# Row gathers of layer 0 recorded at other places: fewer beside the latent heads' inverses and second scan, more beside the dense experts and the attention projections

## The chip, the core and the metric

The kernel runs on one core of a Trainium2 chip. The metric is device microseconds (us) of one execution; the median of three executions is 4625.11 us (4613.94 to 4629.98). The program has five instruction streams: TensorE (PE, with its weight loads PEld), VectorE (DVE), ScalarE (ACT), GpSimd (POOL) and SyncE (SP). Each stream runs its instructions in the order in which they stand; streams wait for each other by semaphores.

## The reference

Two layers over 512 latent tokens and 256 context tokens, width 1024. Layer 0 mixes with a bidirectional gated DeltaNet, layer 1 with windowed attention, and each ends with a PEER expert retrieval:

```python
for i in range(DEPTH):
    y, yc = gdn_mixer(...) if i % 2 == 0 else swa_mixer(...)
    x = x + g1 * y
    x = x + g2 * peer_ffn(modulate(x, ...), w_query, sub_keys, expert_u, expert_v)
    if not last:
        xc = xc + cg1 * yc
        xc = xc + cg2 * peer_ffn(modulate(xc, ...), ...)
return rmsnorm(x, final_g)

def peer_ffn(h, ...):              # 8 heads x 16 experts = 128 of 16384 experts for each token
    idx, gate = top_k(...)         # from two products with 128 sub-keys each
    act = gelu(einsum('pkd,pd->pk', expert_u[idx], h)) * gate
    return einsum('pk,pkd->pd', act, expert_v[idx])
```

## The kernel before

Tokens stand in tiles of 128: two of context, four of latents. The experts of a tile are computed in one of two ways. **Dense** tiles (three of layer 0, two of layer 1) run through all 16384 experts as matrix products: `ups` makes `pu` (lines 84 to 86, three matmuls for one product because weights are split into a high and a low part), `dense` multiplies by gate tables `G` and makes `pv`. The split of a weight tile is a cast on ACT (line 295, `wh`) and a subtraction on DVE (line 296, `wl`). Dense work goes in 16 **superblocks**: each has eight products `pu` (the last two superblocks have none, since `pu` runs 16 products ahead) and 16 weight tiles of `pv`, and ends with six adds into `acc` (line 1328).

**Gathered** tiles (both context tiles and one latent tile of layer 0, two of layer 1) fetch the chosen experts only. One gather is an indirect DMA of 128 rows, 512 KB, issued by POOL. A tile needs 128 gathers of `u` (line 1184; each is multiplied with the tokens by one DVE instruction, line 1186) and then 128 of `v` (line 1211). Four `v` gathers make a **group**: DVE builds a selection `W` (line 1204) and PE adds the four into `po` by eight matmuls (line 1218; the profiler shows 16). When a tile's last group is done, `finish` copies `po` to `gacc` (line 1223), scales it, adds it to the stream `xf` (lines 1132 and 1133) and stores it to `xl` in memory (line 1135). The second context tile's `v` are two works, of 20 and of 12 groups (`CUT = 20`); the latent tile's come between them.

Gathers are recorded between other work: `self.back` lists gather works, and a call `self.tick(n, mix)` adds `n` to a debt and records gathers until the debt is paid, `u` and `v` by turns as `mix` says. The table `TICK` holds `n` for each place:

```python
self.tick(TICK["inv"][h0 // 4], MIX["inv"][h0 // 4])      # 8 times in each latent half
self.tick(TICK["scan"][h0 // 4], MIX["scan"][h0 // 4])    # 32 times in each latent half
self.tick(TICK["u", l], MIX["dense"])                     # before each of 112 products pu
self.tick(TICK["v", l], MIX["dense"])                     # 128 times, once for a weight tile of pv
self.tick(TICK["swa"], MIX["swa"])                        # attention projections, 6 per tile
done()                                                    # = drain: records all gathers that are left
norm(0, 2, 1)                                             # context tiles, before columns(4, ...)
```

A scheduler then orders all instructions by recording order and by when they can start. Recording order is a priority: a gather that found no free row buffer is put behind later work. There are six row buffers for both kinds (`RING`), five more in the dense stage of layer 0 (`MORE`).

The order of the program around the change: context heads, then the latent heads in two halves (`gdn_units`: gates and decay matrices, 31 steps of a block inverse on DVE at lines 574 and 576, inverse products at line 598, scan at lines 657 to 682), output projection (`gdn_out`, `py`), routing of four tiles (`peer_route`, `pq` and top-k), the first 16 products `pu`, gate tables (`gates_dram`, `pg`, line 1263), the dense stage, then attention (`swa`): norm of the latents, projections `pj`, norm of the context, scores.

Of the kernel before, what the change touches and what calls it, by code (L numbers as in the profile page):

```python
# [51 lines left out]
DELTA = 0  # L52
PIN = 1
ADA = 8
TICK = {"norm": 0, "proj": 0, "z": (0, 0), "mat": (0, 0), "inv": (4, 5), "scan": (1, 4), "out": 2, "swa": 6, "route": {"c": 0, "a": 0, "bf": 0, "b": 0}, "gates": (1, 2),
        ("u", 0): 2.1, ("v", 0): 1.9, ("u", 1): 2.2, ("v", 1): 2}

MIX = {"proj": "uv", "z": ("uv", "uv"), "norm": "uv", "mat": ("uv", "uv"), "inv": ("uv", "uv"), "scan": ("uv", "uv"), "out": "v", "swa": "v", "route": "v", "gates": "V", "dense": "uv"}

# [5 lines left out]
class Kern:  # L65
# [355 lines left out]
    def gdn_z(self, si, ns, hi, lo, p, ps, pt, bufs, raw):  # L421
# [5 lines left out]
        for n in ns:  # L427
            zw = [self.wsplit(p, A["g_z"][n, i], "w", [4, 256], raw, 2) for i in range(2)]
            for t in range(NT):
                pz = ps.tile([128, 512], F32, name="pz", tag=pt, bufs=bufs)[:, 0:256]  # L430
                for k in range(KT):
                    s = slice(t * 128, (t + 1) * 128)
                    zh, zl = zw[k // 4]
                    self.mm3(pz, hi[:, k, s], lo[:, k, s], zh[:, k % 4, :], zl[:, k % 4, :], k == 0, k == KT - 1)
                self.tick(TICK["z"][ns[0] // 2], MIX["z"][ns[0] // 2])
                zz = p.tile([128, 2, 128], F32, name="zz", tag="zz", bufs=2)
# [51 lines left out]
    def gdn_units(self, si, h0, HB, S, OD, side, ps, tags):  # L488
# [30 lines left out]
        with ExitStack() as c2:  # L519
            pr = c2.enter_context(self.pool(f"gr{si}{h0}", side))  # L520
            KQ = load(self.KQ, "kq", pr, 2)
            for gi in range(HB // NH):
# [9 lines left out]
                def decay(d, lm, rm, neg):  # L532
                    rr = pr.tile([128, 4, 128], F32, name="rr", tag="rr", bufs=2)
                    for i, h in enumerate(heads):
                        for t in range(NT):
                            nc.scalar.mul(rr[:, i * NT + t, :], rm, V["g"][:, t, 8 * d + h:8 * d + h + 1])
                    pe = bank("pe", "pe")
                    mm(pe, lm, rr, start=True, stop=False)
                    mm(pe, self.identb, neg[:, None, :].to_broadcast([128, 4, 128]), start=False, stop=True)
                    E = pr.tile([128, 4, 128], F32, name="E", tag="E", bufs=2)  # L540
                    nc.scalar.activation(E, pe, AF.Exp)
                    return E
# [9 lines left out]

                self.tick(TICK["mat"][h0 // 4], MIX["mat"][h0 // 4])
                Ef = decay(0, self.m_gt, self.m_le, self.neg_gt)
# [29 lines left out]
        with ExitStack() as c2:  # L584
# [5 lines left out]
            for g4 in range(NU // 4):  # L590
# [9 lines left out]

                self.tick(TICK["inv"][h0 // 4], MIX["inv"][h0 // 4])
                D4, a4, b4 = ([X[:, u, :] for u in us] for X in (Dm, ta, tb))
# [29 lines left out]
        for step, hh in [(st, hg + i) for hg in range(0, HB, 4) for st in range(NT) for i in range(4)]:  # L632
            h = h0 + hh
            for d in range(2):
                t = step if d == 0 else NT - 1 - step
                u = d * (NU // 2) + hh * NT + t
                inv = (tb if d == 0 else ta)[:, u, :]
                self.tick(TICK["scan"][h0 // 4], MIX["scan"][h0 // 4])
                s = slice(t * 128, (t + 1) * 128)
# [90 lines left out]
    def out_proj(self, wsrc, gate, p, ps, pt, bufs, resident, plain=False):  # L730
# [11 lines left out]
        def run(tiles):  # L742
# [3 lines left out]
            for n in range(4):  # L746
# [3 lines left out]
                for x, (y, _, xout) in zip(xs, tiles):  # L750
                    py = ps.tile([128, 512], F32, name="py", tag=pt, bufs=bufs)[:, 0:256]
                    for k in range(KT):
                        self.mm(py, [i[:, k] for i in y], [w[:, k % 4, :] for w in W[n][k // 4]], k == 0, k == KT - 1)
                    self.tick(TICK["out"], MIX["out"])
                    gy = p.tile([128, 256], F32, name="y", tag="oy", bufs=3)
# [8 lines left out]
    def swa(self, xl, gate, xout, done, free):  # L764
# [3 lines left out]
        with ExitStack() as ctx:  # L768
# [6 lines left out]
            with ExitStack() as c1:  # L775
# [19 lines left out]
                def columns(n, tiles):  # L795
                    w = [self.wsplit(p, A["s_in"][n, i], "w", [4, 256], 2, 2) for i in range(2)]
                    Q = {}
                    for t in tiles:
                        s = slice(t * 128, (t + 1) * 128)
                        pj = ps.tile([128, 256], F32, name="pj", tag="pj", bufs=3)  # L800
                        for k in range(KT):
                            wh, wl = w[k // 4]
                            self.mm3(pj, hi[:, k, s], lo[:, k, s], wh[:, k % 4, :], wl[:, k % 4, :], k == 0, k == KT - 1)
                        self.tick(TICK["swa"], MIX["swa"])
                        if n == 5:
# [766 lines left out]
```

## Time and profile before

| | |
|---|---|
| median of 3 executions | 4625.11 us |
| profiled execution, its own time | 4615.7 us |
| its span, first to last instruction | 4613.9 us |
| PE, DVE, ACT, POOL busy | 84%, 68%, 39%, 38% |
| bytes moved by DMA | 1258.59 MB |
| of them by POOL's queue (gathers, mostly) | 712.07 MB |

Busy PE time is modelled and matmuls overlap, so 84% is not the share of a peak. What counts is the stage: from the latent heads to the attention projections the program passes through stretches in which DVE, PE or the DMA engines are full in turn.

### The profile page before, as it was taken

What the parts mean: (1) busy time and instruction counts of PE and PEld (TensorE: products, weight loads), DVE (VectorE), ACT (ScalarE), POOL (GpSimd) and SP (SyncE); (2) the same over time, 40 slices, a digit from 0 to 9 for tenths busy, and PEclk for the clock granted to TensorE, in tenths of its full rate; (3) what the DMA queues carried; (4) which work ended last, traced back from release to release, by engine and by line L of the source; (5) the groups of instructions that cost most, each with busy time, mean ns of one, the idle gap of its engine ahead of it and who ended that gap; (6) DMA issues with size and microseconds to landing.
All of it is one profiled execution on the core that took longest, in us unless ns stands there. A gap on an engine that the chain in (4) does not pass through costs nothing.

```text
span 4613.9 us, 65361 instructions
## 1 busy us (share of the span) xinstructions
PE 3888.7 (84%) x23123; PEld 3126.8 (68%) x23123; DVE 3153.7 (68%) x7853; ACT 1789.2 (39%) x3428; POOL 1749.3 (38%) x1463
## 2 busy tenths in 40 slices
PE   7989989647798879999999997897956778888997
PEld 5867778545577668777877775765845666666665
DVE  4663469976699888666853344665898996767634
ACT  4754563413235633322332223443336332333322
POOL 0000011654345362465643340000340766656553
PEclk9989999878899989999999998998978899999999
DMA  6725553768798997899988883201255999999998
GB/s 237 245 86 184 206 186 109 283 242 310 283 319 280 305 375 273 326 393 367 379 326 320 329 321 138 78 19 70 82 187 157 392 365 395 406 396 409 400 398 338
DMA packets 432904, 1258.59 MB, mean 273 GB/s; under 512 B 40640, under 2 KB 139840, under 8 KB 432576
## 3 DMA queue, kind: packets, MB, share of 16 engines
q0 software_dynamic: 195968, 712.07, 40.8%
q1 hardware_dynamic: 236608, 542.34, 32.9%
q8 instruction: 182, 2.98, 0.3%
q14 instruction: 146, 1.20, 0.1%
HBM read 1176.66 MB, written 77.59 MB: 272 GB/s over the span
## 4 chain that ended last, share of the span: by engine, by line
PE 47%; DVE 22%; DMA 12%; issue 7%; ACT 4%; POOL 2%; SPq 0%; DVEq 0%; ACTq 0%; POOLq 0%
PE pv L84 5%; PE pv L85 5%; PE po L1218 5%; DMA u<-p_u,idx 5%; PE pv L86 5%; DVE u L1186 4%; PE pu L86 4%; PE pu L84 4%; PE pu L85 4%; DVE wl L296 3%; DMA v<-p_v,idxT 3%; DVE oa L1254 1%; ACT wh L295 1%; PE pg L1263 1%; DVE ob L1261 1%
## 5 line engine op out<-in xcount | busy, mean ns | idle before, releaser
L1184 POOL DMA_INDIRECT u<-p_u,idx x640 | 844.3, 1319 | 712.8 <-DVE u L1186 157.2
L296 DVE TENSOR_TENSOR wl<-w,wh 128x1024 fp32r<-128x1024 f32 x604 | 737.0, 1223 | 422.1 <-ACT wh L295 411.8
L1211 POOL DMA_INDIRECT v<-p_v,idxT x640 | 729.9, 1140 | 747.2 <-PE po L1218 426.5
L295 ACT CAST wh<-w 128x1024 fp32r<-128x1024 f32 x636 | 659.2, 1046 | 885.9 <-PE pu L85 222.8
L1186 DVE SCALAR_TENSOR_TENSOR u<-u,hg 128x1024 f32<-128x1024 f32 x640 | 770.4, 1223 | 198.9 <-DMA u<-p_u,idx 196.3
L84 PE MATMUL pu<-lo,wh 128*128 128x384 f32 (+1 forms) x2048 | 658.4, 321 | 80.6 <-ACT a L1282 50.9
L86 PE MATMUL pu<-hi,wl 128*128 128x384 f32 (+1 forms) x2048 | 657.8, 321 | 48.3 <-DVE wl L296 43.0
L85 PE MATMUL pu<-hi,wh 128*128 128x384 f32 (+1 forms) x2048 | 650.6, 318 | 0.0
L84 PE MATMUL pv<-wl,ah 128*128 128x512 f32 x1280 | 525.0, 410 | 97.8 <-DVE wl L296 93.1
L85 PE MATMUL pv<-wh,ah 128*128 128x512 f32 x1280 | 510.4, 399 | 0.0
L86 PE MATMUL pv<-wh,al 128*128 128x512 f32 x1280 | 507.9, 398 | 0.0
L84 PEld LDWEIGHTS pu<-lo,wh 128*128 128x128 f32 x2048 | 407.0, 199 | 125.9 <-ACT a L1282 65.5
L86 PEld LDWEIGHTS pu<-hi,wl 128*128 128x128 f32 x2048 | 406.7, 199 | 65.9 <-DVE wl L296 54.6
L85 PEld LDWEIGHTS pu<-hi,wh 128*128 128x128 f32 x2048 | 406.5, 198 | 7.7 <-issue 6.7
L84 PEld LDWEIGHTS pv<-wl,ah 128*128 128x128 f32 x1280 | 246.5, 193 | 229.8 <-DVE wl L296 126.4
L1218 PE MATMUL po<-v,W 128*32 128x512 f32 x2560 | 322.7, 618 | 43.9 <-DMA v<-p_v,idxT 43.8
L86 PEld LDWEIGHTS pv<-wh,al 128*128 128x128 f32 x1280 | 246.2, 192 | 59.0 <-issue 4.2
L1282 ACT ACTIVATE a<-pu 128x384 f32<-128x384 f32 (+1 forms) x256 | 110.8, 434 | 442.0 <-PE pu L86 434.8
L96 ACT CAST ah<-a 128x384 fp32r<-128x384 f32 (+1 forms) x256 | 116.6, 460 | 422.3 <-PE pv L85 379.6
L85 PEld LDWEIGHTS pv<-wh,ah 128*128 128x128 f32 x1280 | 247.1, 193 | 49.0 <-issue 0.8
L296 POOL TENSOR_TENSOR wl<-w,wh 128x1024 fp32r<-128x1024 f32 x32 | 78.8, 2472 | 514.1 <-ACT wh L295 467.5
L1263 PE MATMUL pg<-oa,ob 128*128 128x128 f32 x1280 | 177.2, 293 | 56.8 <-DVE oa L1254 32.7
(485 smaller groups left out, 7139.2 us busy)
## 6 DMA issues: line engine op xcount, KB each, us to landing
w<-p_ut SPq DMA_DIRECT2D x256, 512.0 KB, 6.7
w<-p_vt SPq DMA_DIRECT2D x256, 512.0 KB, 6.8
w<-adaw SPq DMA_DIRECT2D x96, 512.0 KB, 5.4
G<-st SPq DMA_DIRECT2D x20, 2048.0 KB, 13.6
w<-g_qkv SPq DMA_DIRECT2D x48, 512.0 KB, 5.1
Gt<-G SPq DMA_DIRECT2D x32, 768.0 KB, 6.8
w<-p_wq SPq DMA_DIRECT2D x32, 512.0 KB, 5.7
Gt<-G SPq DMA_DIRECT2D x32, 512.0 KB, 6.8
```

The lines of the kernel that those rows point to most:

```text
L84: mm(out, lh, rl, start=start, stop=False)
L85: mm(out, lh, rh, start=False, stop=False)
L86: mm(out, ll, rh, start=False, stop=stop)
L96: self.nc.scalar.copy(hi, x)
L295: nc.scalar.copy(hi, w)
L296: (sub or nc.vector).tensor_sub(lo, w, hi)
L1184: nc.gpsimd.indirect_dma_start(out=u, out_offset=None, in_=A["p_u"], in_offset=bass.IndirectOffsetOnAxis(ap=idx[:, s:s + 1], axis=0))
L1186: pin(nc.vector.scalar_tensor_tensor(u, u, 1.0, h, op0=OP.mult, op1=OP.mult, accum_out=w[:, s:s + 1]))
L1211: nc.gpsimd.indirect_dma_start(out=v, out_offset=None, in_=A["p_v"], in_offset=bass.IndirectOffsetOnAxis(ap=idxT[:, t:t + 1], axis=0))
L1218: pin(nc.tensor.matmul(po[hf][32 * g:32 * g + 32, :], W[:, g, :], vs[g][:, hf * 512:(hf + 1) * 512], start=j == j0, stop=j == j1 - 1, tile ...
L1263: nc.tensor.matmul(pg[:, :, j], ob[:, j, :], oa[:, j, :], start=True, stop=True)
L1282: nc.scalar.activation(a.rearrange("p g t -> p (g t)"), pu, AF.Gelu)
```

## The change

Two lines of the table change. In the latent heads each tick of the inverse products asks for 3 and 3 gathers (4 and 5 before) and each tick of the scans for 1 and 2 (1 and 4 before). In the dense stage of layer 0 a `pu` asks for 2.2 (2.1) and a weight tile of `pv` for 2.1 (1.9). No arithmetic is added or removed, and the same 768 gathers of layer 0 are made.

```diff
-TICK = {"norm": 0, "proj": 0, "z": (0, 0), "mat": (0, 0), "inv": (4, 5), "scan": (1, 4), "out": 2, "swa": 6, "route": {"c": 0, "a": 0, "bf": 0, "b": 0}, "gates": (1, 2),
-        ("u", 0): 2.1, ("v", 0): 1.9, ("u", 1): 2.2, ("v", 1): 2}
+TICK = {"norm": 0, "proj": 0, "z": (0, 0), "mat": (0, 0), "inv": (3, 3), "scan": (1, 2), "out": 2, "swa": 6, "route": {"c": 0, "a": 0, "bf": 0, "b": 0}, "gates": (1, 2),
+        ("u", 0): 2.2, ("v", 0): 2.1, ("u", 1): 2.2, ("v", 1): 2}
```

The layer-0 ticks from the latent heads to the output projection ask for 72 + 160 + 32 = 264 gathers before and 48 + 96 + 32 = 176 after; those of the dense stage for 478 and 515.

Where the scheduler puts the instructions that use the rows was counted in both built programs. `u` are counted as DVE instructions of line 1186, groups of `v` as sets of eight matmuls of line 1218:

| place | `u` before | `u` after | groups before | groups after |
|---|---|---|---|---|
| latent heads, both halves | 128 | 128 to 130 | 1 | 0 |
| output projection | 15 | 6 to 8 | 3 | 5 |
| norm and routing, first 20 `pu` | 37 | 0 | 17 | 5 |
| gate tables | 0 | 0 | 11 | 12 |
| superblocks 0 and 1 | 67 | 35 | 0 | 8 |
| superblocks 2, 3, 4, 5 | 9, 15, 22, 22 | 25, 40, 20, 10 | 0, 3, 5, 6 | 2, 0, 0, 1 |
| superblocks 6, 7, 8 | 17, 24, 28 | 21, 21, 23 | 4, 2, 1 | 6, 5, 6 |
| superblocks 9, 10 | 0, 0 | 29, 24 | 8, 8 | 2, 2 |
| superblocks 11, 12, 13 | 0 | 0 | 8, 7, 9 | 9, 9, 8 |
| superblocks 14, 15 | 0 | 0 | 3, 0 | 4, 5 |
| attention projections | 0 | 0 | 0 | 7 |

The first place is POOL's stream around the second latent half (`ta`, `tb`, `X` are buffers of its inverse; `x_...` is a buffer of its inverse products). Before:

```order
L514 MEMSET ta 128x4096
L515 MEMSET tb 128x4096
L1184 DMA u<-p_u,idx 128x1024 x24
L566 MEMSET X 128x1024
L567 MEMSET X 128x32
L1184 DMA u<-p_u,idx 128x1024 x22
L589 MEMSET x_9042 128x512
```

And in the changed kernel:

```order
L514 MEMSET ta 128x4096
L515 MEMSET tb 128x4096
L1184 DMA u<-p_u,idx 128x1024 x24
L566 MEMSET X 128x1024
L567 MEMSET X 128x32
L1184 DMA u<-p_u,idx 128x1024 x12
L589 MEMSET x_9018 128x512
```

Ten gathers moved from the block inverse to behind the last row shown; from there to the first `v` there are 53 `u` before and 63 after, so the heads end with the same number.

The second place is DVE's stream in the routing: the top-k (`top`, `ti`, `wk`, `sc`) of one query product for four tiles, with the weight split `wl`. Before:

```order
L1004 MATCH_REPLACE wk<-top_11131,sc 128x128
L1005 MAX top_11130<-wk 128x8
L1186 SCALAR_TENSOR_TENSOR u,gw<-u,hg 128x1024
L1005 MAX top_11131<-wk 128x8
L1006 MAX_INDEX ti_11134<-top_11130,wk 128x8
L296 TENSOR_TENSOR wl<-w,wh 128x1024
L1006 MAX_INDEX ti_11135<-top_11131,wk 128x8
L1002 MAX top_11128<-sc 128x8
```

And in the changed kernel:

```order
L1004 MATCH_REPLACE wk<-top_10801,sc 128x128
L1005 MAX top_10800<-wk 128x8
L1005 MAX top_10801<-wk 128x8
L1006 MAX_INDEX ti_10804<-top_10800,wk 128x8
L1006 MAX_INDEX ti_10805<-top_10801,wk 128x8
L296 TENSOR_TENSOR wl<-w,wh 128x1024
L1002 MAX top_10798<-sc 128x8
```

No `u` product stands in the routing any more.

The third place is ACT's stream from the end of the dense stage into the projections: `gacc` is the second context tile's sum, `junk` the squares of the norm of a tile (`x_25208` and `x_25209` are the two context tiles in both programs), `Q`, `qT` copies of projections. Before:

```order
L1223 COPY gacc<-po 128x512 x2
L96 CAST ah<-a 128x384 x2
L295 CAST wh<-w 128x1024
L96 CAST ah<-a 128x384 x2
L295 CAST wh<-w 128x1024
L96 CAST ah<-a 128x384 x2
L295 CAST wh<-w 128x1024 x6
L255 ACTIVATE junk,ss<-x_24423 128x1024
L255 ACTIVATE junk,ss<-x_24424 128x1024
L255 ACTIVATE junk,ss<-x_25208 128x1024
L255 ACTIVATE junk,ss<-x_24425 128x1024
L255 ACTIVATE junk,ss<-x_25209 128x1024
```

And in the changed kernel:

```order
L809 COPY Q<-pj 128x256 x3
L1223 COPY gacc<-po 128x512 x2
L295 CAST wh<-w 128x1024
L809 COPY Q<-pj 128x256
L295 CAST wh<-w 128x1024
L837 COPY qT<-ptq 64x512 x2
L255 ACTIVATE junk,ss<-x_25209 128x1024
L257 ACTIVATE r<-ss,eps 128x2
L272 ACTIVATE hk<-pt,col_77 128x256 x2
```

The second context tile's sum moved from the dense stage behind the third copy of the fourth projection, and the norm that needs it stands a few instructions behind. On PE, 18 matmuls of `pj` and 8 transposes of `Q` stand between that tile's last group and the first transposes of the context norm; behind those come the projections of the context.

## Rows read from the trace of the kernel before

**Rows 1.** The page: busy time of the engines, and GB/s in 40 slices.

```profile
PE 3888.7 (84%) x23123; PEld 3126.8 (68%) x23123; DVE 3153.7 (68%) x7853; ACT 1789.2 (39%) x3428; POOL 1749.3 (38%) x1463
...
GB/s 237 245 86 184 206 186 109 283 242 310 283 319 280 305 375 273 326 393 367 379 326 320 329 321 138 78 19 70 82 187 157 392 365 395 406 396 409 400 398 338
```

**Rows 2.** Busy time of each engine in stretches of the program (us).

```profile
core 0: us, PE busy (x) PEld busy (x) DVE busy (x) ACT busy (x) POOL busy (x), PEclk, DMA share, GB/s
920.00:976.00 56.00, 14.08 (x96) 13.88 (x96) 49.47 (x106) 7.73 (x12) 24.56 (x20) 0.62 0.61 214
1018.00:1103.00 85.00, 59.19 (x373) 51.45 (x371) 76.22 (x204) 32.38 (x107) 47.80 (x40) 0.84 0.82 291
1103.00:1231.00 128.00, 85.71 (x408) 62.48 (x408) 64.28 (x145) 39.20 (x114) 41.32 (x41) 0.80 0.85 314
1231.00:1340.00 109.00, 104.28 (x538) 79.38 (x538) 96.64 (x444) 28.90 (x42) 52.37 (x50) 0.97 0.88 313
1340.00:1460.00 120.00, 118.59 (x715) 98.54 (x713) 117.70 (x550) 48.93 (x70) 64.38 (x48) 1.00 0.87 303
1460.00:1622.00 162.00, 128.21 (x950) 101.54 (x950) 138.60 (x377) 113.22 (x299) 65.04 (x45) 0.95 0.91 294
1622.00:1791.90 169.90, 128.75 (x605) 112.07 (x603) 139.01 (x224) 51.62 (x77) 101.66 (x74) 0.90 0.98 368
1791.90:1859.30 67.40, 65.73 (x326) 60.02 (x326) 64.15 (x159) 25.55 (x36) 0.57 (x1) 0.97 0.50 167
1791.90:2104.00 312.10, 296.04 (x1553) 244.89 (x1554) 227.44 (x407) 95.89 (x132) 149.18 (x123) 0.99 0.87 331
2104.00:2336.20 232.20, 218.98 (x1119) 186.81 (x1119) 176.59 (x265) 72.75 (x102) 140.33 (x102) 0.98 0.95 363
...
2336.20:2749.60 413.40, 413.40 (x2322) 315.84 (x2321) 169.44 (x233) 119.17 (x163) 161.16 (x166) 1.00 0.88 328
2749.60:2823.30 73.70, 71.16 (x333) 54.04 (x331) 33.41 (x41) 18.95 (x24) 11.17 (x21) 1.00 0.50 174
2789.70:2823.30 33.60, 31.77 (x141) 25.97 (x139) 12.91 (x15) 5.27 (x5) 7.01 (x14) 1.00 0.27 96
2823.30:2860.00 36.70, 6.21 (x32) 4.38 (x32) 16.44 (x22) 20.61 (x33) 0.00 (x0) 0.61 0.43 161
2860.00:2955.00 95.00, 92.16 (x733) 89.87 (x734) 50.62 (x187) 32.49 (x66) 0.00 (x0) 0.97 0.17 56
3224.80:3328.50 103.70, 102.48 (x493) 86.28 (x494) 76.86 (x484) 31.61 (x48) 34.93 (x15) 0.97 0.25 81
```

**Rows 3.** DVE's costliest groups from 1231 to 1460.

```profile
L296 DVE TENSOR_TENSOR wl<-w,wh 128x1024 fp32r<-128x1024 f32 x35 | 42.6, 1218 | 1.7 <-ACT wh L295 1.7
L1186 DVE SCALAR_TENSOR_TENSOR u<-u,hg 128x1024 f32<-128x1024 f32 x32 | 38.9, 1216 | 11.4 <-DMA u<-p_u,idx 11.4
```

**Rows 4.** The chain from 1460 to 1622: one group (start us, us).

```profile
1514.17 1.85 PE po L1218 x16
```

**Rows 5.** Waits from 1103 to 1231: total us, times, longest.

```profile
DVE u L1186 <- DMA u<-p_u,idx: 26.9, 10, 5.9
...
PE po L1218 <- DMA v<-p_v,idxT: 22.4, 2, 17.6
```

**Rows 6.** Gathers in the table of DMA issues: count, median us to landing.

```profile
u<-p_u,idx POOLq DMA_INDIRECT x640, 8.3
v<-p_v,idxT POOLq DMA_INDIRECT x640, 7.9
```

**Rows 7.** The chain from the last add of the dense stage into the norm.

```profile
2825.44 1.22 DVE acc L1132
...
2827.71 1.23 DVE xf L1133
...
2831.79 7.14 DMA x<-xl
...
2840.19 1.28 ACT L257
```

## The prediction

> **What bounds the kernel now.** The page first [rows 1]: PE is busy 84% of the span, DVE 68%, POOL 38%, and the GB/s line moves between 19 and 409. No engine is full all the time, so I read the stages one by one in the table of busy times by stretches [rows 2]. The program has a different limit in each.
>
> In the second half of the latent heads DVE is the limit: 49.5 of 56 us before the inverse products and 76.2 of 85 in the scan. In the output projection and the norm (1103 to 1231) nothing is full; the waits there [rows 5] are for gathers: 26.9 us of DVE for `u`, 22.4 us of PE for `v`, one of them 17.6. In the routing (1231 to 1460, 229 us) DVE and PE are both full: 96.6 + 117.7 = 214.3 and 104.3 + 118.6 = 222.9. Among DVE's costliest groups stand 32 `u` products, 38.9 us and 11.4 of waiting [rows 3]. In the gate tables DVE leads (138.6 of 162). In the dense stage PE leads: 413.4 of 413.4 in superblocks 9 to 13, 219.0 of 232.2 in 6 to 8, 296.0 of 312.1 in 2 to 5. In 6 to 8 the DMA share is 0.95 too. The attention projections are PE again, 92.2 of 95 us, with the DMA engines at 0.17.
>
> So rows cost a different engine in each place. A `u` is 1.22 us of DVE [rows 3], about 1.3 with what it adds between instructions (my choice). A group of `v` is 1.85 us of PE in the chain [rows 4]; the dense stage gives the same: superblock 2 has no group and takes 67.4, so (413.4 - 5 x 67.4) / 40 groups = 1.91 [rows 2].
>
> **The change part by part.** The counts are those of the table of places above. The heads end with the same number of rows; what leaves is the routing's share, and what gains is the dense stage and the projections.
>
> *Heads.* Ten `u` leave the block inverse, a place where DVE is nearly full: -13. They come in the scan, as full: +13. Sum 0, bounds -13 (the scan's 9 idle us hide most of them) to +6.
>
> *Output projection and norm.* Some eight `u` of 15 go, and with them part of 26.9 us of waits; two groups more come, and the long `v` wait stays, since POOL still issues the first `v` behind the last `u`. I take -6; bounds -15 (more than half of the `u` waits) and +3 (the two groups, with no wait saved).
>
> *Routing.* DVE's 214.3 us shed 32 x 1.3 = 42 and fall to about 172, and 11.4 of waits go too. PE becomes the floor. Layer 1's routing has the same matmuls without groups and takes 103.7, 102.5 of it PE [rows 2]. The 480 `pu` matmuls (20 products) are priced by the difference of a superblock with and without its 192: (67.4 - 33.6) / 192 = 0.176, so 84.5. Three groups that stay behind the norm are 5.7. Sum 194; with the loose ends of the present stage (229 - 223 = 6) some 199: **-30**. Bounds -15 (the `pu` still wait for `wl`, whose 35 subtractions stand in DVE's order) and -35 (the floor).
>
> *Gate tables.* 12 groups for 11, no `u`: 0.
>
> *Superblocks 0 and 1 with their lead* (1622 to 1791.9, 169.9 us; PE 128.8, DVE 139.0, DMA share 0.98): eight groups come (+15), 32 `u` go. This stretch waits for rows and tables, not for an engine, so fewer rows (67 before, 35 + 32 after) is no change in bytes. I take +3; bounds -10 and +10.
>
> *Superblocks 2 to 15* are the heart. PE's floors before are 296.0, 219.0, 413.4 and 71.2 [rows 2] against 312.1, 232.2, 413.4 and 73.7: 32 us of excess, 29 of it in the seven superblocks that hold all 137 `u`. That is 0.21 us of loss for a `u` on top of what hides beside PE. After the change the same stretch has 213 `u` and 59 groups instead of 64.
> - 2 to 5: 14 groups become 3 (-21), 68 `u` become 95. But they lump: superblock 3 gets 40, and DVE there needs 33 (a superblock of 9 to 13, with no `u`, takes it 169.4 / 5 = 34 with its groups' selections) + 40 x 1.3 = 85, over PE's 67; superblock 2 gets 25 and 4 gets 20, the latter beside the pair sums of routing, some 71 and 77 with the excess. With 69 for superblock 5 the sum is 302; the ring's waits add 8: 310, **-2**.
> - 6 to 8: 7 groups become 17, and rows 69 + 28 = 97 become 65 + 68 = 133. The window moved 363 GB/s x 232.2 us = 84.3 MB [rows 2]; 36 rows of 0.524 MB make it 103. The fastest slices of the page are 392 to 409 GB/s [rows 1], so 103 MB takes some 258 at 399: **+26**. The engines alone would give +19 (ten groups), or 0 if rows come early.
> - 9 and 10: 16 groups become 4 (-23), 53 `u` come (+13): **-10**.
> - 11 to 13: 24 groups become 26: **+4**. 14 and 15: 3 become 9: **+11**, as PE is full there (71.2 of 73.7).
>
> Sum about **+27** with rounding; bounds -10 (floor alone: 5 groups fewer at 1.91, `u` at nothing) and +45 (every lump at its worst).
>
> The Trainium skill, in "DMA: Bandwidth & Descriptors", section "Issuing engines are not separate DMA queues", says that transfers issued by different engines share the same 16 DMA engines and interleave there. By that rule gathers that move into the dense stage delay its weight tiles. The trace agrees so far: the DMA share there is 0.87 to 0.98 [rows 2], while the routing that loses rows has 0.87.
>
> The same page's section on bandwidth gives about 358 GB/s for a core's memory side; by that estimate 103 MB would take 288 us, 56 more than now. The trace disagrees: 363 over a whole window [rows 2].
>
> *Attention projections.* Seven groups more at 1.91 are +13, for PE is busy 92.2 of 95. Then the second context tile ends here and no longer before the norm. Its tail is a copy, scale and add (1.22 + 1.23), store and load (7.14), and squares, root and scale (1.28 and two more), all rows of the like tail of the latents [rows 7]: some 17 us. Behind its last group PE has 26 short instructions, at 92.2 / 733 = 0.126 each some 3.3, with their weights up to 6. So 11 us of waiting are new. The 28 rows themselves arrive by a ring of six with 7.9 to 8.3 us to land [rows 6]: five rings, most of it beside the norm (36.7 us, DMA share 0.43); I add 1. Sum **+25**; bounds +5 (the groups run in the norm, where PE is busy 6.2 of 36.7) and +32.
>
> Sum: 0 - 6 - 30 + 0 + 3 + 27 + 25 = **+19**. The profiled execution took 4615.7, so it would take 4635. The three runs lie 1.8 below to 14.3 above it; the mean of the four is 4621.2, and on that the changed kernel takes 4640.
>
> **The rivals.** (1) *Faster.* The excess of superblocks 2 to 8 belongs to the gathers' transfers and not to DVE, which is busy only 227 of 312 and 177 of 232 there. Then what counts there is how many rows PE waits for, the lumps of `u` lie beside PE's work, and the stretch goes with PE's floor (-10), and the sum is 0 - 6 - 30 + 3 - 10 + 25 = -18: 4603. For it: PE is busy 0.95 of 2 to 5 already with `u` beside it, and groups (1.9 us of the full engine) drop by five. Against it: the lumps of 40 and of 17 groups. It decides when the dense term is below some -6. (2) *No change.* The seven groups and the context's tail hide in the norm and in the first projections (term +5 rather than +25): sum 0, about 4621. For it: PE has 30 idle us in the norm; against it: PE's order has the last group behind the third part of the fourth tile's projections. (3) *Bound by the DMA engines.* The dense term is +45 and the routing gives only 22: 4665. For it: a share of 0.95 to 0.98 already; against it: superblocks 9 to 13, at 0.88 and 328 GB/s, lose rows of `v`.
>
> **How the numbers follow.** Runs of before differ by 0.3% (16 us), so that is about what can be told from no change: 13.9 us either way. Chances: the sum as worked out 0.33, the DMA case 0.18, no change 0.25, faster 0.24. Most of the first case is slower by more than 0.3%, part of it (0.07) within; its own range is 4625 to 4655. From these cases: slower 0.45, same 0.29, faster 0.26. The range runs from 4600 (the faster case) to 4670 (the DMA case).
>
> **What would show it.** In the profile after: the routing some 199 us long with no `u` and PE idle under 10 us; superblock 3 long (85) with DVE full; superblocks 6 to 8 at 258 with a DMA share over 0.95; the projections about 120 us with a wait of PE of 10 us or more ahead of the context's transposes. I am wrong if the routing stays at 229, which means that `wl` or weights set it and not the rows; if 2 to 8 take 528 or less, which is rival 1; or if the projections stay near 100.

## The result, and the profile after

The changed kernel takes 4650.36 us (median, 4646.31 to 4661.81) against 4625.11: a ratio of 1.0065, 95% interval 1.005 to 1.008. It is slower by some 30 us. Forecast were 4640 us, and slower with a chance of 0.45. The profiled execution has a span of 4644.5, 30.6 more than before.

The page of the changed kernel, against [rows 1]:

```profile
PE 3896.6 (84%) x23123; PEld 3130.6 (67%) x23123; DVE 3154.9 (68%) x7853; ACT 1786.2 (38%) x3426; POOL 1757.1 (38%) x1463
...
GB/s 247 243 89 191 218 161 104 306 214 331 250 109 231 337 376 351 311 310 388 378 363 348 333 322 229 114 19 69 82 191 143 377 381 384 400 409 409 386 408 328
```

The engines are as busy as before, to 8 us. Only the line of GB/s shows where the change is: the slice with 319 before, in the routing, has 109, and the two slices from the end of the dense stage on have 229 and 114 where 138 and 78 stood.

Busy time by stretches of the changed kernel, the same stages as [rows 2] (the second scan, output projection, routing, gate tables, superblocks 0 and 1, 2 to 5, superblock 3 alone, 6 to 8, 9 and 10, 11 to 13, 14 and 15, norm, projections):

```profile
core 0: us, PE busy (x) PEld busy (x) DVE busy (x) ACT busy (x) POOL busy (x), PEclk, DMA share, GB/s
...
1001.30:1098.00 96.70, 64.38 (x346) 54.42 (x345) 84.55 (x214) 32.08 (x103) 62.63 (x48) 0.80 0.85 308
1098.00:1218.50 120.50, 87.94 (x445) 62.93 (x443) 53.51 (x130) 39.95 (x115) 37.37 (x39) 0.84 0.86 318
1218.50:1415.70 197.20, 192.18 (x1043) 170.88 (x1043) 176.43 (x920) 76.38 (x112) 14.57 (x15) 0.99 0.44 145
1415.70:1578.60 162.90, 131.74 (x965) 103.43 (x966) 135.95 (x375) 111.13 (x295) 66.88 (x46) 0.93 0.87 283
1578.60:1751.50 172.90, 141.63 (x718) 111.77 (x717) 104.13 (x166) 51.00 (x76) 88.54 (x75) 0.90 0.95 362
1751.50:2055.80 304.30, 283.11 (x1402) 246.39 (x1400) 256.53 (x452) 97.64 (x135) 154.51 (x112) 0.97 0.86 324
1826.00:1911.20 85.20, 75.46 (x359) 67.73 (x359) 77.04 (x121) 23.92 (x33) 62.86 (x41) 0.92 0.98 373
2055.80:2312.20 256.40, 242.16 (x1279) 191.32 (x1280) 171.78 (x262) 70.42 (x96) 159.04 (x132) 0.99 0.98 379
2312.20:2475.40 163.20, 146.77 (x730) 124.87 (x729) 126.62 (x192) 49.01 (x69) 103.11 (x75) 0.95 0.98 373
2475.40:2727.70 252.30, 252.30 (x1432) 189.56 (x1435) 100.72 (x142) 70.77 (x97) 99.88 (x104) 1.00 0.90 334
2727.70:2812.50 84.80, 82.98 (x428) 56.94 (x420) 34.69 (x47) 18.75 (x24) 35.03 (x45) 1.00 0.77 284
2812.50:2855.40 42.90, 7.07 (x32) 5.07 (x32) 14.95 (x19) 19.30 (x30) 5.74 (x6) 0.55 0.54 199
2855.40:2981.50 126.10, 107.70 (x842) 94.81 (x843) 56.84 (x199) 34.72 (x70) 23.98 (x25) 0.91 0.44 151
```

The stages side by side, their ends taken from the two traces:

| stage | before | after | difference | forecast |
|---|---|---|---|---|
| end of the first latent half's scan to the second half's inverse products | 114.7 | 105.5 | -9.2 | -13 |
| inverse products, second scan | 124.4 | 138.2 | +13.8 | +13 |
| to the routing | 130.5 | 122.4 | -8.1 | -6 |
| routing | 229.4 | 197.2 | -32.2 | -30 |
| gate tables | 161.6 | 162.9 | +1.3 | 0 |
| superblocks 0 and 1 | 169.9 | 172.9 | +3.0 | +3 |
| superblocks 2 to 5 | 312.1 | 304.3 | -7.8 | -2 |
| superblocks 6 to 8 | 232.3 | 256.4 | +24.1 | +26 |
| superblocks 9 and 10 | 165.4 | 163.2 | -2.2 | -10 |
| superblocks 11 to 13 | 247.9 | 252.3 | +4.4 | +4 |
| superblocks 14 and 15 | 73.7 | 84.7 | +11.0 | +11 |
| norm and projections | 131.6 | 169.3 | +37.7 | +25 |

These sum to some 36. Ahead of the first row the changed kernel's profile is 9.0 us earlier. Of these, 8.4 us are there at the first inverse products of layer 0, long before the first gather of either program (817 and 807), and the other profiles of this study scatter there too (from 336.1 to 345.1). Behind the last row it is 4 us later. For the whole the ratio counts.

The chain of the changed kernel at the end of its last group (start us, us, what):

```profile
2921.36 1.85 PE po L1218 x16
2923.22 0.32 PE pj L84
2924.16 1.06 ACT wh L295
...
2926.38 0.65 DVE gacc L1132
...
2929.28 1.14 DVE xf L1133
...
2930.71 3.44 DMA xl<-xf
2934.17 3.29 DMA x<-xl
2937.48 1.16 ACT junk L255 x2
...
2939.19 0.76 DVE x L260
2940.09 1.10 PE pt L269 x4
```

From the last group's end to the context's first transposes are 17 us; TensorE works 3.7 of them and stands idle 5.3 and 7.9. That is 13.2 of the 31.5 by which the projections are longer; seven groups of 1.9 are 13.3, and the waits for rows are these (engine, line, releaser: total, times, longest, over norm and projections):

```profile
PE pt L269 <- DVE x L260: 36.4, 2, 28.5
...
PE ptq L831 <- DVE Q L824: 5.3, 1, 5.3
PE po L1218 <- DMA v<-p_v,idxT: 4.4, 3, 2.6
```

The first of them holds the latents' norm (28.5) and the context's (7.9). The norm itself is 6.2 longer. The DMA issues of that stretch in the changed kernel (KB each, median us to landing):

```profile
x<-xl SPq DMA_DIRECT2D x5, 512.0 KB, 10.0
xl<-xf SPq DMA_DIRECT2D x3, 512.0 KB, 6.3
...
v<-p_v,idxT POOLq DMA_INDIRECT x6, 9.4
```

And in the kernel before:

```profile
x<-xl SPq DMA_DIRECT2D x6, 512.0 KB, 5.5
xl<-xf SPq DMA_DIRECT2D x3, 512.0 KB, 3.1
```

Six rows, one round of the ring, are on their way while the latents are stored and loaded again, and those transfers take about twice as long (medians of the landings that the traces show).

### The profile page after: what moved, and what is told of

Same layout as the page of the kernel before. It is cut to its first block, busy times and chain, and to the rows that moved or that the text cites. A ratio compares the mean times of both kernels' runs of the same rounds, so it can differ in the third digit from the quotient of the medians.

```text
span 4644.5 us, 65384 instructions
## 1 busy us (share of the span) xinstructions
PE 3896.6 (84%) x23123; PEld 3130.6 (67%) x23123; DVE 3154.9 (68%) x7853; ACT 1786.2 (38%) x3426; POOL 1757.1 (38%) x1463
## 4 chain that ended last, share of the span: by engine, by line
PE 47%; DVE 21%; DMA 16%; issue 6%; ACT 4%; POOL 1%; SPq 0%; DVEq 0%; ACTq 0%; POOLq 0%
DMA v<-p_v,idxT 5%; DMA u<-p_u,idx 5%; PE pv L84 5%; PE po L1218 5%; PE pv L85 4%; PE pv L86 4%; DVE u L1186 4%; PE pu L86 4%; PE pu L84 4%; PE pu L85 4%; DVE wl L296 3%; ACT wh L295 1%; DVE oa L1254 1%; DMA w<-p_vt 1%; PE pg L1263 1%
## 5 line engine op out<-in xcount | busy, mean ns | idle before, releaser
L1184 POOL DMA_INDIRECT u<-p_u,idx x640 | 863.9, 1350 | 683.9 <-DVE u L1186 157.4
L1211 POOL DMA_INDIRECT v<-p_v,idxT x640 | 718.0, 1122 | 956.9 <-PE po L1218 608.8
```

Of the source, the lines that this page charges most:

```text
L1184: nc.gpsimd.indirect_dma_start(out=u, out_offset=None, in_=A["p_u"], in_offset=bass.IndirectOffsetOnAxis(ap=idx[:, s:s + 1], axis=0))
L1211: nc.gpsimd.indirect_dma_start(out=v, out_offset=None, in_=A["p_v"], in_offset=bass.IndirectOffsetOnAxis(ap=idxT[:, t:t + 1], axis=0))
```

## The experiments

Every kernel was timed against the kernel before on its own chip; a ratio is to that. A stage's time is that of one profiled execution, which lies up to 13.5 us off its kernel's median. `no_tail` and `late_after` below have the changed kernel's dense stage, and their superblocks 2 to 15 took 1064.0 and 1062.8 us for 1060.9, so some 3 us between two kernels in a stage mean nothing. Rows of `u` and groups are counted in the traces, by where their instructions ran (the expectations count in the built programs, which can differ by a few).

**Which half of the change.** Three kernels take a part of the change each, and a fourth makes the dense ticks high enough that nothing is left for the projections. The four edits are shown against the changed kernel.

`heads_only`:

```diff
-        ("u", 0): 2.2, ("v", 0): 2.1,
+        ("u", 0): 2.1, ("v", 0): 1.9,
```

> Only the heads' ticks of the change (3, 3 and 1, 2); the dense ticks stay at 2.1 and 1.9. In the built program the routing has no u product, and 17 groups instead of 7 come to stand in the attention projections. Theory (in the projections a group costs a round of the six row buffers, about 9.7 us as in the changed kernel's trace, not 1.9 us of TensorE): 17 x 9.7 = 165 us from the first projection, the context's tail 17 us behind, so 75 us slower than the changed kernel and 105 us slower than before. Rival (a group costs the 1.9 us of TensorE wherever it stands): the dense stage gains what the projections lose, as the changed kernel, +30 us over before.

4682.85 us, ratio 1.0123 (1.0106 to 1.014): +57, between the two. The projections did as the theory says. Norm and projections took 255 us, 86 more than in the changed kernel; 12 groups stand in the projections, one every 10 us, and POOL waits there for row buffers (who waited for the tile `po`: us, times):

```profile
  POOL v L1211: 89.5, 11
```

The five groups of the latent tile end in the norm, with 39.8 us of idle TensorE behind them. What failed is the other side: superblocks 2 to 15, which lost ten groups to the norm and the projections, took 1010.5 us against 1061.0. That is 5 us for each group that left, and not 1.9, but it is no price of a group: superblocks 2 to 5, 9 and 10, which lost one group and eight `u` between them, gave 28 of the 50 us, and 11 to 13, which lost seven groups and got 13 `u`, gave 14. The `u` are spread another way there (32 in superblock 3 and 14 in 9, for 40 and 29).

`dense_more`:

```diff
-        ("u", 0): 2.2, ("v", 0): 2.1,
+        ("u", 0): 2.6, ("v", 0): 2.3,
```

> The changed kernel with higher dense ticks (2.6 and 2.3 for 2.2 and 2.1): the heads and the routing as in the changed kernel, no group left for the attention projections, the last one in superblock 15. Theory (38 of the changed kernel's loss is the projections, and a group in the dense stage costs 1.9 us): +30 - 38 + 7 x 1.9 and a few us of crowding = +8 us over before, between 0 and +18. Rival (the dense stage is full of transfers, and 28 rows more cost there what they cost in the projections): +30 us over before.

4635.25 us, ratio 1.002 (1.001 to 1.003): +9, the theory's +8. Its norm and projections are those of the kernel before, 37.3 and 94.9 us. The routing took 198.7. So the 38 us of the changed kernel's attention belong to the seven groups, and the dense stage asks some 21 for them.

`inv_only`:

```diff
-"scan": (1, 2),
+"scan": (1, 4),
```

> Only the inverse products' ticks changed (3, 3 for 4, 5) and the dense ticks of the change; scans as before. The routing keeps 15 u products of 28 and 13 groups of 16; no group in the projections. Theory (a routing u costs what DVE loses, 1.3 us, until TensorE's groups set the end): routing -13 us, dense stage +8 by two groups and 20 u more, -2 elsewhere: -7 us against before, between -15 and +5. Rival (the routing is set by weights or by wl, and loses nothing until all u are gone): +5 us.

4641.85 us, ratio 1.0037 (1.0023 to 1.0051): +17, and both are wrong. The routing, from the first `pq` to the first `pg`, has the theory's -13 in number: 214.9 us for 229.4. But 43 of its 480 matmuls of `pu` ran behind the first `pg`, and the gate tables took 7.4 longer. These matmuls in the gate tables (TensorE's busy time first; before and in the changed kernel there are none):

```profile
1439.90:1609.20 169.30, 8.38 (x45) 7.33 (x43) 0.00 (x0) 0.94 0.87 282
```

The two stages together gained 7 us, and TensorE's three groups less are 5.8 of them; the twelve `u` products less gave next to nothing. What the theory priced at 8 is more: superblocks 0 and 1 took 9.1 longer, superblocks 6 to 8 30 (262.1 for 232.3). Sixteen `u` more in superblocks 2 to 15, with the same 64 groups, cost 28 us there. At 0.524 MB each and the 359 GB/s that 6 to 8 moved, their bytes alone are 23 us. (The profiled execution is 8 us over the median of this kernel.)

`scan_only`:

```diff
-"inv": (3, 3),
+"inv": (4, 5),
```

> Only the scans' ticks changed (1, 2 for 1, 4) and the dense ticks of the change; inverse products as before. The routing has no u and 8 groups (the changed kernel 3, before 16); one group stands in the projections. Theory: routing -22 us (five groups more than the changed kernel's -32), dense stage +20, the one group hidden with its tail beside the latents' projections +2, so 0 us against before, between -10 and +12. Rival (one group left is enough to put the second context tile's tail on the path): +17 us more.

4643.91 us, ratio 1.0047 (1.0032 to 1.0062): +22. The routing is right again (-24.6); the dense stage took 37 more and not 20, and one group left in the projections costs 9.4, half of the rival's price (the norm 5.9 longer, the projections 3.5).

The four routings make a series (busy time from `pq` to `pg`; `inv_only`, then `scan_only`):

```profile
1225.00:1439.90 214.90, 206.78 (x1160) 168.47 (x1161) 201.29 (x978) 74.83 (x114) 83.61 (x75) 0.99 0.79 273
```

```profile
1233.60:1438.40 204.80, 203.82 (x1123) 174.08 (x1124) 177.00 (x927) 74.11 (x114) 34.68 (x35) 0.99 0.55 188
```

With the `u` and groups of each: 32 and 16 take 229.4 us, 20 and 13 take 214.9 (and 8 outside), 0 and 8 take 204.8, 0 and 3 take 197 to 201 in six kernels. TensorE is busy all but 1 us with 0 and 8: its groups are the floor, as the prediction had it. They are the gain as well. Of the 32.2 us between the two kernels 25.0 are TensorE's matmuls `po` (before, then changed; the first busy time is TensorE's):

```profile
1231.00:1460.40 229.40, 30.78 (x256) 6.68 (x256) 0.00 (x0) 0.00 (x0) 0.99 0.88 308
1218.50:1415.70 197.20, 5.77 (x48) 1.25 (x48) 0.00 (x0) 0.00 (x0) 0.99 0.44 145
```

**What a row costs in the dense stage: its bytes, or its work.** Half a row for every gather of layer 0, in both kernels (`v` the same way; the matmuls read the half twice):

```diff
+            half = self.last is None
-            nc.gpsimd.indirect_dma_start(out=u, out_offset=None, in_=A["p_u"],
+            nc.gpsimd.indirect_dma_start(out=u[:, 512:1024] if half else u, out_offset=None,
+                                         in_=A["p_u"].rearrange("n (a d) -> (n a) d", a=2) if half else A["p_u"],
...
+                pin(nc.vector.scalar_tensor_tensor(
+                    u.rearrange("p (a d) -> p a d", a=2), u[:, None, 512:1024].to_broadcast([128, 2, 512]), 1.0,
```

> The kernel before, but every gather of layer 0 fetches half a row (256 KB of 512): u products, selections, matmuls and POOL's issues stay as many and as long, on the wrong data. The scheduler, which knows the transfer is shorter, puts 8 u and 12 groups into the routing (28 and 16 before). Theory (from the output projection to superblock 8 the rows' bytes set the time where the DMA share is 0.94 and more): superblocks 2 to 15 fall from 1031 to PE's floor, about 1000; gap and superblocks 0 and 1 from 170 to 150; routing 17 less, waits of the projections 15 less: -85 us. Rival (rows cost DVE and TensorE, not transfers): only the waits for rows and the routing go, -30 us, and superblocks 4 to 8 stay at 77 to 85 us each.

> The changed kernel with the same halving of layer 0's gathers (half the bytes, the same instructions, wrong data). Seven groups stay in the attention projections. Theory (transfers): superblocks 2 to 15 fall from 1061 to about 1000 (59 groups at 1.9 on 876 without any, and 10 us of DVE where 34 u meet in one superblock); gap and superblocks 0 and 1 -20; projections -10, as the round of six rows shortens and the norm's loads have the DMA engines for themselves; in all 100 us under the changed kernel, -70 us against before, and within 15 us of the halved kernel before. Rival (DVE and TensorE): superblock 6 to 8 stay at 85 us each, -25 us against the changed kernel, +5 against before.

`half_before`: 4608.07 us, ratio 0.9939 (0.9917 to 0.996), -28. `half_after`: 4613.34 us, ratio 0.9947 (0.9929 to 0.9964), -25. Neither theory holds whole. The difference of the two kernels shrinks from 30 us to some 4, which is the transfer theory's; its sums of -85 and -70 are far off, and -28 is the rival's sum for `half_before` (-30). But superblocks 4 to 8 of `half_before` took from 64 to 87 us and not 77 to 85, as the rival had it, and 6 to 8 of `half_after` took 89, 76 and 74 and not 85 each.

Superblocks 2 to 5 and 6 to 8 of `half_after`:

```profile
1744.10:2051.70 307.60, 288.02 (x1457) 248.92 (x1458) 264.85 (x471) 98.75 (x136) 181.32 (x127) 0.97 0.73 242
2051.70:2290.60 238.90, 229.53 (x1217) 186.90 (x1210) 160.18 (x243) 70.38 (x96) 140.58 (x118) 0.98 0.77 255
```

With the DMA share down from 0.98 to 0.77, 6 to 8 are 17.5 us shorter, and 2 to 5 are 3 us longer. These two can't be read alone, as the scheduler moved work from one to the other: 6 to 8 have 13 groups for 16, and 2 to 5 have 7 for 4. Over superblocks 2 to 10 both have 24 groups, and 211 and 213 `u`; there half the bytes gave 27.4 us (696.5 for 723.9). What the change costs with whole rows, and what with half rows (changed kernel less kernel before, us):

| stage | whole rows | half rows |
|---|---|---|
| superblocks 2 to 8 | +16.3 | +12.0 |
| superblocks 9 and 10 | -2.2 | -15.4 |
| superblocks 11 to 15 | +15.4 | +15.9 |
| norm and projections | +37.7 | +23.5 |

In both columns superblocks 2 to 8 go from 21 groups to 20 and from some 136 `u` to 160, and 9 and 10 from 16 groups to 4 and from no `u` to some 52. So about 17 of the 29.5 us that superblocks 2 to 15 lost go with half the bytes, 13 of them in 9 and 10, where the DMA share of the changed kernel is 0.98. In 6 to 8 the share is 0.98 too, but what grew there is mostly TensorE's work for groups. Its matmuls `po` in 6 to 8, with whole rows before and after, then with half rows before and after:

```profile
2104.00:2336.20 232.20, 13.46 (x112) 2.92 (x112) 0.00 (x0) 1.16 (x2) 0.98 0.95 363
2055.80:2312.20 256.40, 33.69 (x256) 7.11 (x256) 0.00 (x0) 0.00 (x0) 0.99 0.98 379
2096.30:2321.80 225.50, 13.47 (x112) 2.93 (x112) 0.00 (x0) 1.17 (x2) 0.98 0.75 249
2051.70:2290.60 238.90, 27.57 (x216) 5.98 (x208) 0.00 (x0) 0.00 (x0) 0.98 0.77 255
```

That is 20.2 of the 24.1 us with whole rows and 14.1 of 13.4 with half. TensorE's waits in superblocks 2 to 10 of `half_after` are for the adds of line 1328 on DVE (25.6 us) and for rows of `v` (8.7), hardly any for split weights (0.2). So with the bytes taken away DVE's order is next. (`half_before` also has 17 `u` more ahead of the routing, and took 22 us longer from the second half's inverse products to the routing; part of the missing gain lies there.)

The other side was tried with the bytes kept and the work left out. `no_product`:

```diff
+        if l == 0 and self.sets > 1:
+            nc.vector.memset(w, 0.5)
...
-            pin(nc.vector.scalar_tensor_tensor(u, u, 1.0, h, op0=OP.mult, op1=OP.mult, accum_out=w[:, s:s + 1]))
+            if l or self.sets < 2:
+                pin(nc.vector.scalar_tensor_tensor(u, u, 1.0, h, op0=OP.mult, op1=OP.mult, accum_out=w[:, s:s + 1]))
```

> The changed kernel without the DVE products of u for the second context tile and the latent tile (256 of layer 0's 384; their rows are still fetched, their weights are set to a constant): the bytes stay, the products that stand on DVE and wait for their rows go. Theory (in superblocks 2 to 10 a product that waits for its row holds up the split wl behind it on DVE, and TensorE waits for wl: 41 us there in the changed kernel): those waits fall under 10 us, superblocks 2 to 10 from 724 to about 683, 50 us under the changed kernel in all, -20 against before. Rival (the transfers set the superblocks): 6 to 8 stay at 83 us or more each, 20 us under the changed kernel, +10 against before.

4652.85 us, ratio 1.0051 (1.0033 to 1.007): +22. The theory falls (-20), and the rival's sum (+10) is missed too; two of the rival's three superblocks are over its 83 us. Superblock 3, with no group and no product of `u`, then superblocks 6, 7 and 8:

```profile
1828.60:1920.40 91.80, 71.77 (x338) 62.90 (x337) 32.73 (x43) 24.79 (x35) 40.19 (x39) 0.91 0.95 374
2060.80:2150.10 89.30, 82.07 (x430) 63.87 (x428) 30.63 (x42) 22.90 (x32) 48.34 (x48) 0.96 0.99 392
2150.10:2243.00 92.90, 85.34 (x436) 66.82 (x437) 33.89 (x46) 23.47 (x33) 50.38 (x51) 0.94 0.99 375
2243.00:2324.10 81.10, 77.08 (x407) 62.45 (x407) 32.22 (x43) 24.00 (x33) 37.06 (x36) 1.00 0.99 382
```

In 6 to 8 DVE fell to 97 us of 263, and the stretch is no shorter (256.4 with the products): they don't set it. Superblocks 2 to 10 took 727 us against 724. TensorE's waits for casts and split weights are no shorter: 56 us, in the changed kernel 47 (superblocks 2 to 10; line numbers are one higher here):

```profile
PE pv L85 <- DVE wl L297: 36.3, 12, 12.3
PE pu L85 <- ACT wh L296: 12.6, 7, 3.5
PE pu L87 <- DVE wl L297: 7.3, 10, 1.6
```

The longest of these waits, 12.3 us, was made by the experiment itself. The pair sums of the latent tile's routing (`pairw`) use one of the row buffers; in superblock 3 ACT and DVE stood still until a row landed there whose product had been left out, and TensorE waited for the split behind it (waits from 1878 to 1908):

```profile
ACT pairw L1087 <- DMA u<-p_u,idx: 18.1, 1, 18.1
DVE pairw L1089 <- DMA u<-p_u,idx: 13.9, 1, 13.9
```

The changed kernel has no such wait. Without it superblock 3 would be some 79 us (an estimate: 91.8 less 12.3), under the 85.2 that it takes with the products, so this run doesn't show that its length comes from transfers. In the changed kernel DVE is busy 77.0 of the 85.2 us there and waits for no row. A superblock of `dense_more` with 39 `u` and fewer bytes, its superblock 3, is DVE's almost alone:

```profile
1857.10:1933.60 76.50, 70.90 (x350) 64.19 (x351) 75.53 (x120) 25.73 (x36) 48.15 (x30) 0.98 0.91 350
```

So DVE's work is some 76 of the 85 us; whether the transfers are the rest isn't shown.

In superblocks 2 to 10 of `no_product` DVE waits 126.7 us for ACT's casts, and DVE, ACT and TensorE all have idle time. The DMA engines are full where 39 to 50 rows a superblock (35 in the eighth) go beside its weights. That the weights come late for that reason is not shown: ACT's casts waited 27.2 us there for weights to land, and 45.4 in the changed kernel.

**What the tail costs.** `no_tail`:

```diff
         if self.last is None:
-            queue.dma_start(xd, x)
+            if not skip:
+                queue.dma_start(xd, x)
             return
...
-        self.finish(xd, acc, gate, p, self.ring, nc.gpsimd)
+        self.finish(xd, acc, gate, p, self.ring, nc.gpsimd, self.last is None and j0 == CUT)
```

> The changed kernel without the store of the second context tile's stream by its last gather work (line 1135 for that work alone; the layer after reads the tile without its second part of the experts). The seven groups stay in the projections, but the norm of the context no longer waits for them. Theory (groups 13, waits for v 4, tail 13, slower norm 6): the tail's 13 us go, 17 us slower than before. Rival (TensorE would have stood there anyway, for rotated Q and for weights): +30 us as the changed kernel.

4653.89 us, ratio 1.0036 (1.0023 to 1.005): +17, as the theory. Its projections took 114.4 us for 126.4.

`late_after` covers the tail and leaves out nothing:

```diff
-                done()
-                norm(0, 2, 1)
-                columns(4, range(6))
-                columns(5, range(6))
+                columns(4, range(2, 6))
+                columns(5, range(2, 6))
+                done()
+                norm(0, 2, 1)
+                columns(4, range(2))
+                columns(5, range(2))
```

> The changed kernel with another order of the attention projections: the latents' fifth and sixth projection (keys and values) come before the context's norm, the context's behind it, for four weight tiles split twice. Nothing else moves; seven groups stay there. Theory (13 us of tail are uncovered in the changed kernel, and eight projections of 3.3 us now cover them): 11 us under the changed kernel, +19 against before. Rival (the second splits stand where the tail stood): +30 as the changed kernel.

4641.92 us, ratio 1.0031 (1.0018 to 1.0044): +14. The projections took 115.0 us; the wait for the context's norm is gone.

**A better table.** If a row costs least where the DMA engines have room, the kernel before should gain from fewer rows in its full superblocks. `slow_s1` is that kernel with one number changed; `late_s2` and `late_s3` go further and take the order of `late_after` as well.

```diff
-        ("u", 0): 2.1, ("v", 0): 1.9,
+        ("u", 0): 2.1, ("v", 0): 1.8,
```

> The kernel before with one number changed: a weight tile of pv in layer 0 asks for 1.8 gathers instead of 1.9. Heads and routing as before; superblocks 14 and 15 get 4 and 2 groups (3 and 0 before), none reaches the projections, and the superblocks before them get 58 instead of 61. Theory (a row costs 1.3 us of transfer in a full superblock and its share of 1.9 us per group in the last two, where the DMA share is 0.50): -5 us, between -12 and +3. Rival (a group costs 1.9 us anywhere): 0 us.

> The heads' ticks of the kernel before, dense ticks 2.0 and 1.8 (before 2.1 and 1.9), and the latents' keys and values before the context's norm. Two groups stand in the projections, 3 in superblock 15, 4 in 14 (before 0, 0 and 3), and the superblocks before them get 53 instead of 61. Theory (a row costs least where the DMA engines have room: the last two superblocks and, once the tail is covered, the projections): 8 groups leave the full superblocks at up to 5 us each, 8 cost 2.5 us, 6 for the slower norm: -8 us against before, between -18 and +4. Rival (1.9 us anywhere, and the norm's 6): +8.

> As the one with dense ticks 2.0 and 1.8, with 2.0 and 1.7: five groups in the projections, 3 in superblock 15, 4 in 14, and 49 in the superblocks before. Theory: 12 groups leave the full superblocks, 12 cost 2.5 us, 6 for the norm, 3 for weights split twice: -8 us against before, between -22 and +6. Rival (1.9 us anywhere, the ring's pace in the projections not covered): +15.

`slow_s1`: 4626.93 us, 0.9985 (0.9969 to 1.0001), -7, not told apart from 0. `late_s2`: 4618.95 us, 0.9969 (0.9955 to 0.9983), -14, faster than both kernels. `late_s3`: 4628.8 us, 0.9984 (0.9969 to 0.9999), -7. In `late_s2` superblocks 2 to 13 took 938.5 us for 957.7, 14 and 15 81.0 for 73.7, norm and projections 144.2 for 131.6. The last two superblocks and the projections:

```profile
2731.90:2812.90 81.00, 79.19 (x396) 56.03 (x386) 32.20 (x43) 17.69 (x22) 28.21 (x36) 1.00 0.63 228
2857.30:2957.10 99.80, 95.84 (x765) 90.69 (x766) 58.80 (x197) 38.20 (x74) 3.56 (x5) 0.97 0.32 106
```

(By a count of the built programs the superblocks ahead of the last two hold 55 and 52 groups in `late_s2` and `late_s3`, not the 53 and 49 of the expectations.) Where the -14 of `late_s2` lies is not shown: these three differences are -19.2, +7.3 and +12.6, about 0 together, as the profiled execution of the kernel before is 9 us under its median. `late_s2` changes ticks and order together, and the order alone was not run on the kernel before.

## Why the prediction was right, point by point

The four signs that it named all came: a routing of 197.2 us without `u`, TensorE idle for 5.0; superblock 3 at 85.2, 77.0 of it DVE's; superblocks 6 to 8 at 256.4 with a DMA share of 0.98; projections of 126 us with 13 us of waits ahead of the context's transposes. The reasons behind them held in part.

*Routing.* -32.2 for -30, by the reason that the sum was built on. TensorE's floor, from layer 1's routing, 20 products and three groups (194, taken as 199), came to 197.2. What the prediction put first, 42 us off DVE, is not what shows: TensorE was the fuller engine before too (222.9 of 229.4), and 25.0 us of the gain are its 13 groups. Of the two kernels between, `scan_only` hit -22 by the same sum (-24.6); `inv_only` hit -13 in number alone.

*Heads and output projection.* -9.2 and +13.8, then -8.1, for -13, +13 and -6: +4.6 where 0 stood for the heads, inside its bounds. Ten products moved from one full place of DVE to another.

*Dense stage.* +29.5 for superblocks 2 to 15. The prediction carried +27, but its five terms add up to +29. Each is within 8 us of what came, and two misses cancel: 2 to 5 came out 5.8 lower, 9 and 10 7.8 higher. For superblock 3 the reason given, DVE's lump of 40 products, accounts for some 76 of the 85.2 us. The term of 6 to 8 is luck: 258 was made from 103 MB at 399 GB/s, and 256.4 came with 97 MB at 379 GB/s, so both figures were too high by about as much. TensorE's groups grew by 20.2 us there, so the price that the prediction set beside it and passed over, +19 for the engines alone, is nearer to what happened. For 9 and 10 -10 was forecast without transfers and -2.2 came; with half the bytes it is -15.4, so there the transfers of the 53 `u` were the part left out. The price of 1.9 us for a group is right in superblocks 11 to 15 (+4.4 and +11.0).

*Projections.* +37.7 for +25, over the bound of 32: the term that was mis-sized. Its parts: groups 13.3 for 13; tail 13.2 for 11 (`no_tail` 12.0, `late_after` 11.4); waits for rows 4.4 for 1; and 6.2 for the norm, where nothing was forecast. The prediction counted the norm as a place where the 28 rows have room and not what six of them do to the norm's own transfers. `scan_only` shows the price alone: one group left, 5.9 us.

*The rivals.* Faster needed the dense term under -6; it was +29.5. No change needed a projections term of +5; 38 came. The DMA case had its reason in part, as 17 of the 29.5 us go with half the bytes, and was too large in its size: the dense stage lost 30 and not 45, since superblocks 4 and 5, with 20 and 10 `u`, became 13 and 11 us shorter.

*The sum.* The stages moved by +36 where +19 stood, and 13 of the 17 us between are the projections. That the time came within 11 us of 4640 owes something to luck: 9.0 us were taken back ahead of the first row, where profiles scatter. The range of 4600 to 4670 holds the rivals' times too, so being inside it says little, and the stages say more. (The chances of the cases add up to 0.44, 0.32 and 0.24 for slower, same and faster, where 0.45, 0.29 and 0.26 stand.)

With six rows beside them the loads of the norm took 10.0 us for 5.5. The Trainium skill, in "DMA: Bandwidth & Descriptors", section "Issuing engines are not separate DMA queues", says that transfers run on the same 16 DMA engines and interleave, whichever engine started them; the traces agree.

Whole stretches moved 379 GB/s over 256 us and 392 over 89. The Trainium skill, in "DMA: Bandwidth & Descriptors", section "Bandwidth", gives the 358 GB/s that the prediction took as a core's share when both cores of a pair stream, and 425 GB/s for one core alone and 16 MB. This kernel runs on one core, and what was measured lies between the two.

What stays open: why sixteen `u` cost 28 us in `inv_only`, where bytes account for 23; what the last 8 or 9 us of superblock 3 are; and how the gain of the halved kernels divides between transfers, DVE's bursts and the places that the scheduler chose for them.

## What to carry to other kernels

When work is moved between stages, price it in each stage by the resource that is full there. Here a group costs some 2 us of TensorE in the routing, in superblocks 6 to 8 and in 11 to 15, and in the routing a `u` beside it cost next to nothing (`inv_only`). Where 40 `u` meet in one superblock most of the price is DVE's, in superblocks 9 and 10 it is the transfers', and in the projections it is a round of the ring. A DMA share of 0.98 did not tell which: it stands in 6 to 8, where half the bytes took 4 us off what the move cost in 2 to 8, and in 9 and 10, where they took off 13. Test a price before you use it: leave out the work and keep the bytes, then halve the bytes and keep the work. Compare stretches that hold the same work, and look for new waits that the test itself makes. And look what hangs on the last piece: one group more past a stage's end lengthened the stage behind it by 9 us, and a reordering of four lines covered the tail.

## What the runs showed that was not expected

Removing either limit alone gave little: without DVE's products superblocks 2 to 10 stayed at 727 us (12 of them a wait that the test made), with half the bytes they fell from 724 to 696.5, of which TensorE was busy 660.

In `heads_only` a group's matmuls took up to 1063 ns against 589 at the least (`po`, line 1218), in the part of the projections where TensorE waited 5 to 7 us for rows before each of five groups. Over that part the granted clock is 0.50, the lower of the two levels (1.2 GHz), where the stretch ahead of it, with TensorE busy 44 of 52 us, has 0.97:

```profile
2917.30:2965.00 47.70, 18.83 (x82) 3.45 (x82) 1.88 (x4) 1.98 (x4) 13.97 (x16) 0.50 0.58 203
```

In that run the stage that waited for rows paid again in the clock.
